# Two transformer blocks on one core: conditioning vectors made by VectorE row sums in place of small matmuls, with one more buffer per weight ring and new pool starts

## The chip, the cores and the metric

The kernel runs on one core of a Trainium2 chip. The metric is device time in microseconds (us), from the first to the last instruction of the core with what lies around it. All arithmetic is float32; TensorE takes its operands as pairs of rounded floats (fp32r).

## The reference, cut to what matters

Two blocks follow each other on 512 tokens of width 1024. The first has two layers; each norm in it is scaled, shifted and gated by six vectors that a matrix product makes from one conditioning row (`c` for the tokens, `c_ctx` for 256 context tokens):

```
sc  = silu(c);  scc = silu(c_ctx)
for l in range(2):
    shift1, scale1, gate1, shift2, scale2, gate2 = split(sc @ w_mod[l] + b_mod[l], 6)    # w_mod[l] is 1024 x 6144
    ...                                       the same six from scc for the context
    xn = rms_norm(x, g_norm1[l]) * (1 + scale1) + shift1
    mix = concat(attention, fourier, conv, pool)(xn @ w_in[l]) @ w_out[l]
    x = x + gate1 * mix
    xn = rms_norm(x, g_norm2[l]) * (1 + scale2) + shift2
    x = x + gate2 * ((silu(xn @ w_a) * (xn @ w_g)) @ w_ffn_out)       # inner width 2816
```

The second block has a retention and convolution layer and a latent attention layer, without conditioning.

## The kernel before, in words

Activations lie transposed: 128 features by up to 512 tokens. Every weight tile is loaded as `raw` (SyncE issues all loads), split into a rounded part `wh` (ScalarE or VectorE) and a rest `wl` (VectorE), and each product is three matmuls (`mm3`): wh with xh, wh with xl, wl with xh. `raw` has a ring of 4 buffers, `wh` and `wl` of 3 each.

The order of all instructions is not written out. The program is recorded as operations with a due time, and a planner (`Rec.order`) lays them out with its own cost figures, due times (`SHIFTS`, `MOD0`, `LATE` and others in `CFG`), penalties for moving an elementwise operation to another engine (`PEN_...`), and the order of the output columns of each projection (`STEPS`). What it lays out is fixed: each engine runs its list in order, and SyncE issues its loads in order.

Conditioning ("modulation") is made in 12 blocks of 512 columns per layer, `mod_block(l, b)`: eight 128x512 pieces of `w_mod` come in (tiles `mraw` or `raw`), and eight matmuls `md<-mraw,scp` with the silu'd conditioning (`scp`, 32 columns, of which two carry data) as the stationary operand write four 32-row strips of one PSUM bank, in two groups of four matmuls each; the profile counts each of these plain fp32 matmuls twice, so a group shows as x8. ScalarE copies the bank (`mrow`), four transposes `md<-cst,mrow` turn it, a VectorE reduce writes `modT`, two more small operations add the bias and make the scale `sclT`. Blocks 0 to 3 of layer 0 come first of all, blocks 4 to 11 of layer 0 during its mixers (`NMOD`), and the 12 of layer 1 during the feed-forward of layer 0 (`ffn`), one after every second inner tile. Block 10 and 11 of a layer are the gate of its feed-forward; the first `fo` result that is added to `x` needs block 10.

The feed-forward makes inner tiles by pairs: `fa` and `fg` products (512 token columns and 256 context columns in layer 0), silu on ScalarE (`ft`), product and split (`hh`, `hl`, `hid`), then the product `fo` for each group of 5 to 8 inner tiles. Names of tiles: `yxh`, `yxl`, `yc` are the normed inputs, `xt` and `ct` the residual streams.

Pools are stacked from the two ends of the on-chip memory: constants, `spt` (365 columns of small parameters), the weight rings and the rings `a` and `b` on one side; `pp` (attention) and then `pa2` (feed-forward) on the other. The starts of the rings follow from the sizes ahead of them: by the built program every tile of the rings `raw`, `wh`, `wl`, `a` and `b` starts 32 bytes past a multiple of 128, those of `pp` and `pa2` 96 bytes past one.

Of the kernel before, what the change touches and what calls it, by code (L numbers as in the profile page):

```python
# [8 lines left out]
F32 = mybir.dt.float32  # L9
# [7 lines left out]
P = 128  # L17
D = 1024
# [32 lines left out]
def win_cols():  # L51
    out = {}
    ar = np.arange
    for c in range(2):
# [17 lines left out]
     'LATEM': 26000.0,  # L72
# [8 lines left out]
     'PEN_PE': (0, 150, None),  # L81
# [10 lines left out]
     'WOE': 3,  # L92
     'WOK': (3, 0, 2, 7, 5, 4, 6, 1),
     'WOS': 7,
# [8 lines left out]
     'PEN_CP': (0, 0, None),  # L103
     'PEN_CZ': (0, 0, None),
     'PEN_PE': (0, 0, None),
# [18 lines left out]
     'PEN_RND': (0, None, None),  # L124
     'PEN_SQ': (None, 0, None),
# [8 lines left out]
     'backlog': 0,  # L134
     'table_slack': 504.2099999999999,
     'urgent': 11068.417919999998},
 3: {'PEN_ADD': (0, None),
     'PEN_AFF': (0, 0, None),
     'PEN_CP': (0, 0, None),
# [15 lines left out]
     'backlog': 0,  # L155
# [2120 lines left out]
```

## Time and profile before

| | |
|---|---|
| median of 3 runs | 2245.21 us (2242.07 to 2246.84) |
| the profiled execution | 2242.23 us, span 2240.2 us |
| TensorE | busy 2134.7 us of the span, 12922 matmul records, mean granted clock 0.98 |
| VectorE, ScalarE | busy 1418.0 and 866.7 us |
| DMA | 258.4 MB, 115 GB/s over the span |

An engine's busy time counts each instruction from its start to its end; matmuls overlap each other, so for TensorE the step from one start to the next says more than the length of one. By stages, all times from the start of the span: the first 56 us load and norm; layer 0's mixers run to about 280, its output projection to about 360, its feed-forward to about 956; layer 1's mixers to about 1120, projection and feed-forward to about 1536; the second block takes the rest.

### The profile page before, as it was taken

The page shows a single profiled execution, that of the slowest core. Times are in us where ns is not written, and L with a number is a line of the kernel's source. Part 1 is how long each engine was busy: PE and PEld are TensorE (multiplying, and loading weights), DVE is VectorE, ACT ScalarE, POOL GpSimd, SP SyncE. Part 2 cuts the span into 40 slices and gives each one's busy share as a digit, 9 for nine tenths or more (in the row PEclk, how much of TensorE's full clock was granted, in tenths as well). Part 3 has the DMA queues.
Part 4 walks back from the last instruction along what each step waited for, and adds up shares of the span by engine and source line. Part 5 has one row for each costly group of instructions (what it writes and reads, how often), then busy time and mean ns, then how long its engine had stood idle before and what let it go on. Part 6 is the DMA issues. An engine that isn't in the chain of part 4 may idle for free.

```text
span 2240.2 us, 32559 instructions
## 1 busy us (share of the span) xinstructions
PE 2134.7 (95%) x12922; PEld 1845.7 (82%) x12922; DVE 1418.0 (63%) x2671; ACT 866.7 (39%) x1646; POOL 22.2 (1%) x35
## 2 busy tenths in 40 slices
PE   7799999999999999888899999999999999999997
PEld 3477799888888888777798888888888888989887
DVE  6998886332232232899984333459775685787996
ACT  6457754111212111664852212215341341435662
POOL 0001000000000000000100000000000000000000
PEclk9799999999999999998999999999999999999998
DMA  8225464222331423422043232335323224543223
GB/s 306 98 98 181 161 217 137 76 98 67 125 101 60 148 78 120 145 89 90 20 142 95 96 110 94 113 117 162 104 85 99 90 89 121 166 139 113 66 77 123
DMA packets 87176, 258.44 MB, mean 115 GB/s; under 512 B 10480, under 2 KB 18160, under 8 KB 87024
## 3 DMA queue, kind: packets, MB, share of 16 engines
q1 hardware_dynamic: 87024, 256.36, 35.7%
q8 instruction: 101, 1.65, 0.3%
q14 instruction: 51, 0.42, 0.1%
HBM read 249.24 MB, written 2.10 MB: 112 GB/s over the span
## 4 chain that ended last, share of the span: by engine, by line
PE 77%; DVE 14%; ACT 4%; DMA 2%; issue 2%; SPq 1%; DVEq 0%; ACTq 0%
PE fa L1001 14%; PE fg L1001 14%; PE fo L1001 13%; PE y L1001 5%; PE wi L1001 5%; PE wo L1001 4%; PE gt L1001 2%; PE egc L1001 2%; PE md L1001 2%; DVE wl L1001 2%; PE ecb L1001 2%; PE ecx L1001 2%; PE ecc L1001 2%; PE egr L1001 2%; DVE cy L1001 1%
## 5 line engine op out<-in xcount | busy, mean ns | idle before, releaser
L1001 DVE TENSOR_TENSOR wl<-raw,wh 128x1024 fp32r<-128x1024 f32 (+5 forms) x387 | 434.6, 1125 | 41.4 <-ACT wh L1001 28.9
L1001 ACT CAST wh<-raw 128x1024 fp32r<-128x1024 f32 (+4 forms) x224 | 216.7, 970 | 417.4 <-PE fo L1001 197.4
L1001 DVE CAST wh<-raw 128x1024 fp32r<-128x1024 f32 (+4 forms) x163 | 105.3, 646 | 211.8 <-PE fa L1001 73.7
L1001 DVE TENSOR_TENSOR ft<-ft,fg 128x256 f32<-128x256 f32 (+1 forms) x66 | 39.4, 598 | 270.7 <-PE fg L1001 270.7
L1001 PE MATMUL fo<-hh,wl 128*128 128x512 f32 (+1 forms) x448 | 156.5, 349 | 6.7 <-DVE wl L1001 6.7
L1001 PE MATMUL fo<-hh,wh 128*128 128x512 f32 (+1 forms) x448 | 157.8, 352 | 0.0
L1001 PE MATMUL fo<-hl,wh 128*128 128x512 f32 (+1 forms) x448 | 157.2, 351 | 0.0
L1001 PE MATMUL fa<-yxh,wh 128*128 128x512 f32 (+1 forms) x384 | 144.9, 377 | 0.0
L1001 PE MATMUL fg<-yxh,wh 128*128 128x512 f32 (+1 forms) x384 | 144.4, 376 | 0.0
L1001 PE MATMUL fa<-yxl,wh 128*128 128x512 f32 (+1 forms) x384 | 143.9, 375 | 0.2 <-DVE yxl L1001 0.2
L1001 PE MATMUL fg<-yxl,wh 128*128 128x512 f32 (+1 forms) x384 | 143.9, 375 | 0.0
L1001 PE MATMUL fa<-yxh,wl 128*128 128x512 f32 (+1 forms) x384 | 142.8, 372 | 0.0
L1001 PE MATMUL fg<-yxh,wl 128*128 128x512 f32 (+1 forms) x384 | 142.7, 372 | 0.0
L1001 PE MATMUL y<-mxh,wl 128*128 128x256 f32 x384 | 110.9, 289 | 6.1 <-DVE wl L1001 6.1
L1001 PE MATMUL y<-mxh,wh 128*128 128x256 f32 x384 | 111.8, 291 | 4.7 <-DVE wh L1001 3.3
L1001 PE MATMUL y<-mxl,wh 128*128 128x256 f32 x384 | 110.1, 287 | 0.3 <-DVE mxl L1001 0.3
L1001 ACT ACTIVATE ft<-fa 128x256 f32<-128x256 f32 (+1 forms) x66 | 34.2, 526 | 178.1 <-PE fa L1001 178.1
L1001 PEld LDWEIGHTS fo<-hh,wl 128*128 128x128 f32 x448 | 85.9, 192 | 18.6 <-DVE wl L1001 7.1
L1001 PEld LDWEIGHTS fo<-hh,wh 128*128 128x128 f32 x448 | 85.4, 191 | 8.4 <-issue 1.7
L1001 PE MATMUL wi<-xxh,wh 128*128 128x512 f32 (+1 forms) x240 | 90.5, 377 | 1.6 <-DVE c L1001 0.7
L1001 PE MATMUL wi<-xxh,wl 128*128 128x512 f32 (+1 forms) x240 | 86.5, 360 | 5.3 <-DVE wl L1001 5.3
L1001 PEld LDWEIGHTS fo<-hl,wh 128*128 128x128 f32 x448 | 86.3, 193 | 5.6
(457 smaller groups left out, 5910.5 us busy)
## 6 DMA issues: line engine op xcount, KB each, us to landing
raw<-in_w SPq DMA_DIRECT2D x291, 512.0 KB, 3.6
mraw<-in_wm SPq DMA_DIRECT2D x48, 512.0 KB, 4.8
raw<-in_wm SPq DMA_DIRECT2D x32, 512.0 KB, 4.8
raw<-in_w SPq DMA_DIRECT2D x24, 448.0 KB, 3.4
raw<-in_w SPq DMA_DIRECT2D x32, 320.0 KB, 3.1
mraw<-in_wm SPq DMA_DIRECT2D x32, 256.0 KB, 5.9
raw<-in_w SPq DMA_DIRECT2D x16, 384.0 KB, 3.1
rw<-rt SPq DMA_DIRECT2D x76, 64.0 KB, 2.0
```

The costliest lines, as they stand in the source:

```text
L1001: getattr(engs[o.eng], method)(*[real(a) for a in args], **{k: real(v) for k, v in kw.items()})
```

## The change

- `mod_rows` replaces `mod_block` for the 12 blocks of layer 1 and for blocks 10 and 11 of layer 0 (`MODV`), which move from the mixers into the feed-forward. The weights of these blocks are stored transposed (`wt`): four tiles of 128 outputs by 1024 inputs for a block. For each, VectorE multiplies the tile by the conditioning row, which lies on all 128 partitions (`crow`, 2 x 1024), and sums along the row: three instructions with a summed output, two of 512 columns for `c` (into `mj`, thrown away) and one of 1024 for `c_ctx`. `crow` is loaded by a broadcast and silu'd by ScalarE when the feed-forward's pool opens. The ring `mraw` of these tiles has one buffer (`NMR`) of 512 KB, where it had two.
- The rings `raw`, `wh` and `wl` have one buffer more (5, 4, 4). The scratch for DMAs issued by GpSimd shrinks to 1 KB per partition; GpSimd issues none.
- Three pads (`spt` 40 columns longer, a 24-column tile on the right side, 544 columns for the wide tiles of `pp`) move the starts: by the built program the rings `raw`, `wh`, `wl`, `a` and `b` now start at multiples of 256 bytes, those of `pp` and `pa2` at odd multiples of 128.
- New settings: due times, penalties, the order in `STEPS` of both layers of the second block, where two projections (`q0`, `t7`) are no longer made in two halves with a load and split of their own each; several others (`k1`, `g5`, `g7`) are made in one piece of 512 columns in place of two of 256.

```diff
 CFG (cut: some twenty values, among them)
-     'LATEM': 26000.0,
+     'LATEM': 25000.0,
-     'WOE': 3,
+     'WOE': 1,
-     'WOS': 7,
+     'WOS': 6,
-     'STEPS': [('q0', '0'), ('g1', '0'), ('k0', '0'), ('g6', 'x'), ('k0', '1'), ('q0', '1'), ('g0', 'x'),
+     'STEPS': [('q0', '01'), ('g1', '0'), ('k0', '0'), ('g6', 'x'), ('g0', 'x'), ('k1', 'x'), ('k0', '1'),
...
+MODP = 10
+MODV = [(0, b) for b in range(MODP, 12)] + [(1, b) for b in range(12)]
...
-    wm = np.stack([inp["w_mod"][l].reshape(2, 4, P, 6144)[..., b].transpose(0, 2, 1, 3)
-                   for l in range(2) for b in MODB])
+    wm = np.stack([inp["w_mod"][0].reshape(2, 4, P, 6144)[..., b].transpose(0, 2, 1, 3) for b in MODB[:MODP]])
+    wt = np.stack([inp["w_mod"][l][:, MODB[b]].T.reshape(4, P, D) for l, b in MODV])
...
-        return self.A(nm=nm) if n <= 512 else self.pp.tile([P, n], F32, tag="w", bufs=4, name=self.name(nm))
+        return self.A(nm=nm) if n <= 512 else self.pp.tile([P, 544], F32, tag="w", bufs=4, name=self.name(nm))[:, :n]
...
-        h = self.pw.tile([P, 1024], F32R, tag="wh", bufs=3, name=self.name("wh"))
-        lo = self.pw.tile([P, 1024], F32R, tag="wl", bufs=3, name=self.name("wl"))
+        h = self.pw.tile([P, 1024], F32R, tag="wh", bufs=4, name=self.name("wh"))
+        lo = self.pw.tile([P, 1024], F32R, tag="wl", bufs=4, name=self.name("wl"))
...
+    def mod_rows(self, l, b):
+        nc = self.nc
+        m4 = self.modT[l][:, b]
+        e = self.col(4)
+        def dot(o, t, c, v, at):
+            nc.vector.scalar_tensor_tensor(o, t[:, c], 1.0, self.crow[:, v, c], op0=ALU.mult, op1=ALU.mult, accum_out=at)
+        for i in range(4):
+            t = self.pa2.tile([P, D], F32, tag="mraw", bufs=self.NMR, name=self.name("mraw"))
+            nc.sync.dma_start(out=t, in_=self.aps["wt"][MODV.index((l, b)), i])
+            o = self.A(nm="mj")
+            dot(o, t, slice(0, 512), 0, m4[:, i, 0:1])
+            dot(o, t, slice(512, D), 0, e[:, i:i + 1])
+            dot(t, t, slice(0, D), 1, m4[:, i, 1:2])
+        nc.vector.tensor_tensor(m4[:, :, 0:1], m4[:, :, 0:1], e.rearrange("p (a o) -> p a o", o=1), op=ALU.add)
+        self.mod_end(l, b)
...
                 if l == 0 and j % 2 == 0 and j < 24:
-                    self.mod_block(1, j // 2)
-                if l == 0 and j % 2 == 1 and self.NMOD + j // 2 < 8:
-                    self.mod_block(0, 4 + self.NMOD + j // 2)
+                    self.mod_rows(1, j // 2)
+                if l == 0 and j % 2 == 1 and MODP + j // 2 < 12:
+                    self.mod_rows(0, MODP + j // 2)
...
+            if self.nph == 2:
+                self.crow = self.pa2.tile([P, 2, D], F32, tag="crow", bufs=1, name="crow")
+                self.nc.sync.dma_start(out=self.crow, in_=self.aps["cr"].rearrange("o (v k) -> o v k", v=2).to_broadcast([P, 2, D]))
+                self.nc.scalar.activation(self.crow, self.crow, AF.Silu)
...
-    NA, NB, NRAW = 53, 11, 4
+    NA, NB, NRAW = 53, 11, 5
+    NA2, NMR = 14, 1
...
-        t = self.psm.tile([P, 8, 2], F32, tag="sc", bufs=1, name="sc")
+        t = self.ptop.tile([P, 24], F32, name="sc")[:, :16].rearrange("p (k v) -> p k v", v=2)
...
-            self.spt = pc.tile([P, nsp], F32, name="spt")
+            self.spt = pc.tile([P, nsp + 40], F32, name="spt")[:, :nsp]
...
-    nc = _bacc.Bacc("TRN2", target_bir_lowering=False, num_devices=1)
+    nc = _bacc.Bacc("TRN2", target_bir_lowering=False, num_devices=1, dynamic_dma_scratch_size=1024)
```

What the planner makes of it shows in three places. On TensorE, in the feed-forward of layer 0, the kernel before puts half a modulation block and its transposes between products of an inner tile (`fa`, `yxh` and `yc` as above):

```order
L1001 MATMUL fa_6117<-yxl_3951,wh_5978 128x512
L1001 MATMUL fa_6117<-yxh_3941,wl_5996 128x512
L1001 MATMUL md_6096<-mraw_6113,scp 32x512 x2
L1001 MATMUL md_6096<-mraw_6129,scp 32x512 x2
L1001 MATMUL fa_6107<-yc_3620,wh_5978 128x256 x2
L1001 MATMUL fa_6107<-yc_3620,wl_5996 128x256
L1001 MATMUL fa_6117<-yxh_3946,wh_5978 128x512
L1001 MATMUL fa_6117<-yxl_3958,wh_5978 128x512
L1001 MATMUL fa_6117<-yxh_3946,wl_5996 128x512
L1001 MATMUL md_1154_6165<-cst,mrow_6160 128x128 x4
L1001 MATMUL fa_6117<-yxh_3964,wh_5978 128x512
```

In the changed program such a stretch holds products alone; no `md` row is left on TensorE after the mixers of layer 0. On VectorE, at the start of that feed-forward, the list before (here the first inner tile) has splits of weights, products and splits of hidden tiles:

```order
L1001 TENSOR_TENSOR ft_4207<-ft_4207,fg_4209 128x256
L1001 TENSOR_TENSOR hid_4360<-ft_4207,hid_4360 128x256
L1001 CAST wh_4378<-raw_4121 128x1024
L1001 TENSOR_TENSOR ft_4334<-ft_4334,fg_4225 128x512
L1001 TENSOR_TENSOR wl_4391<-raw_4121,wh_4378 128x1024
L1001 TENSOR_TENSOR hl_4404<-ft_4334,hh_4396 128x512
```

The changed list has row sums among them, here two tiles of block 11 of layer 0:

```order
L1004 SCALAR_TENSOR_TENSOR mj_4784,modT_306<-mraw_4759,crow 128x512
L1004 TENSOR_TENSOR ft_4719<-ft_4719,fg_4715 128x512
L1004 SCALAR_TENSOR_TENSOR mj_4784,c_4796<-mraw_4759,crow 128x512
L1004 TENSOR_TENSOR wl_4803<-raw_4399,wh_4786 128x1024
L1004 TENSOR_TENSOR hl_4813<-ft_4719,hh_4801 128x512
L1004 SCALAR_TENSOR_TENSOR mraw_4759,modT_306<-mraw_4759,crow 128x1024
L1004 SCALAR_TENSOR_TENSOR mj_4854,modT_306<-mraw_4831,crow 128x512
L1004 SCALAR_TENSOR_TENSOR mj_4854,c_4796<-mraw_4831,crow 128x512
L1004 TENSOR_TENSOR wl_4871<-raw_4466,wh_4856 128x1024
L1004 SCALAR_TENSOR_TENSOR mraw_4831,modT_306<-mraw_4831,crow 128x1024
```

The sums stand wherever the planner found VectorE free by its own figures: the first 4 tiles during the output projection, 16 more ahead of the first `ct<-fo`, the other 36 over the rest of the feed-forward. On SyncE the loads of that stretch alternate:

```order
L1004 DMA mraw_4633<-in_wt 128x1024
L1004 DMA raw_4669<-in_w 128x768
L1004 DMA mraw_4696<-in_wt 128x1024
L1004 DMA raw_4731<-in_w 128x768
L1004 DMA mraw_4759<-in_wt 128x1024
```

Each `mraw` load waits for the last sum of the tile before it, and the weight load that follows stands behind it. In the program before, two `mraw` loads stand together and then three or four weight loads.

## Rows read from the trace of the kernel before

**Rows 1.** Busy time by stage: PE, PEld, DVE, ACT, POOL busy (instructions), clock, DMA.
```profile
56.00:280.00 224.00, 199.75 (x1179) 156.03 (x1178) 200.96 (x454) 140.05 (x275) 13.32 (x14) 0.92 0.40 134
280.00:392.00 112.00, 110.25 (x894) 103.62 (x894) 82.87 (x166) 55.59 (x113) 0.00 (x0) 1.00 0.54 177
392.00:896.00 504.00, 504.00 (x2909) 424.75 (x2909) 149.11 (x228) 90.92 (x144) 0.00 (x0) 1.00 0.29 97
1512.00:2240.00 728.00, 696.37 (x4428) 630.17 (x4426) 549.81 (x1048) 292.33 (x594) 0.00 (x0) 0.98 0.36 110
```
**Rows 2.** PE in time, half a block: start us, us, engine, line, operation, tiles, count.
```profile
451.02 0.39 PE L1001 MATMUL fa<-yxh,wl 128*128 128x512 f32 x1
451.34 1.07 PE L1001 MATMUL md<-mraw,scp 128*32 128x512 f32 x8
452.34 0.50 PE L1001 MATMUL fa<-yxh,wh 128*128 128x512 f32 x1
452.68 0.39 PE L1001 MATMUL fa<-yxl,wh 128*128 128x512 f32 x1
452.91 0.40 PE L1001 MATMUL fa<-yxh,wl 128*128 128x512 f32 x1
```
**Rows 3.** PE in time, the four transposes of a block.
```profile
442.53 0.39 PE L1001 MATMUL fg<-yxh,wl 128*128 128x512 f32 x1
442.76 0.60 PE L1001 MATMUL md<-cst,mrow 128*128 128x128 f32 x4
443.12 0.48 PE L1001 MATMUL fg<-yxh,wh 128*128 128x512 f32 x1
443.43 0.39 PE L1001 MATMUL fg<-yxl,wh 128*128 128x512 f32 x1
```
**Rows 4.** Tile md from 290 to 910 us: count, duration ns min/median/max, first and last start.
```profile
L1001 PE MATMUL md<-mraw,scp x192: 592/605/617, 297.4 to 905.0; 128*32 128x512 f32 x192
L1001 PE MATMUL md<-cst,mrow x48: 270/272/275, 335.1 to 907.0; 128*128 128x128 f32 x48
```
**Rows 5.** DVE by line and form: count, busy us, mean ns of one, idle before.
```profile
L1001 DVE TENSOR_TENSOR wl<-raw,wh 128x1024 fp32r<-128x1024 f32 x291 | 354.7, 1221 | 17.0 <-ACT wh L1001 5.6 <-DVE wh L1001 0.5
L1001 DVE TENSOR_TENSOR hl<-ft,hh 128x512 fp32r<-128x512 f32 x44 | 30.1, 684 | 0.0
L1001 DVE RECIPROCAL c<-c 128x1 f32<-128x1 f32 x72 | 11.0, 154 | 2.8 <-ACT pe L1001 2.6
```
**Rows 6.** ACT, tile c: how ScalarE writes a summed output.
```profile
L1001 ACT ACTIVATION_READ_ACCUMULATOR pe<-sc,c,rq x40: 186/192/233, 166.2 to 1121.9; 128x1 f32 x40
```
**Rows 7.** DMA issues: count, KB each, median us from issue to landing.
```profile
raw<-in_w SPq DMA_DIRECT2D x291, 512.0 KB, 3.6
mraw<-in_wm SPq DMA_DIRECT2D x48, 512.0 KB, 4.8
```
**Rows 8.** What PE waited for: us in total, times, longest.
```profile
PE fo L1001 <- DVE wl L1001: 11.1, 3, 4.3
PE y L1001 <- DVE wl L1001: 6.1, 4, 2.2
PE wi L1001 <- DVE wl L1001: 5.3, 2, 4.1
PE y L1001 <- DVE wh L1001: 3.3, 2, 1.6
PE lat L1001 <- DVE wl L1001: 2.7, 1, 2.7
```
**Rows 9.** PE in time, feed-forward of layer 1: steps of 512-column products from two rings.
```profile
1239.64 0.39 PE L1001 MATMUL fg<-yxh,wh 128*128 128x512 f32 x1
...
1241.91 0.39 PE L1001 MATMUL fa<-yxl,wh 128*128 128x512 f32 x1
...
1299.87 0.40 PE L1001 MATMUL fo<-hh,wh 128*128 128x512 f32 x1
...
1301.50 0.40 PE L1001 MATMUL fo<-hl,wh 128*128 128x512 f32 x1
```

More of the change, by code (lines that the diff above doesn't have):

```diff
@@ L80 @@
      'PEN_CZ': (0, 0, None),
-     'PEN_PE': (0, 150, None),
+     'PEN_PE': (0, 0, None),
      'PEN_RND': (0, None, None),
@@ L102 @@
      'PEN_CA': (0, None),
-     'PEN_CP': (0, 0, None),
+     'PEN_CP': (300, 0, None),
      'PEN_CZ': (0, 0, None),
-     'PEN_PE': (0, 0, None),
+     'PEN_PE': (0, 300, None),
      'PEN_RND': (0, 1000, None),
@@ L123 @@
      'PEN_PE': (0, 0, None),
-     'PEN_RND': (0, None, None),
-     'PEN_SQ': (None, 0, None),
+     'PEN_RND': (0, 150, None),
+     'PEN_SQ': (300, 0, None),
      'PEN_SUB': (0, None),
@@ L128 @@
      'PEN_WL': (0, None),
[5 rows of a table removed]
-     'backlog': 0,
-     'table_slack': 504.2099999999999,
-     'urgent': 11068.417919999998},
[5 rows of a table added]
+     'backlog': 1.5,
+     'table_slack': 2722.7339999999995,
+     'urgent': 29884.72838399999},
  3: {'PEN_ADD': (0, None),
-     'PEN_AFF': (0, 0, None),
-     'PEN_CP': (0, 0, None),
+     'PEN_AFF': (0, 300, None),
+     'PEN_CP': (0, 300, None),
      'PEN_PE': (0, 0, None),
@@ L145 @@
      'PEN_WL': (0, None),
[7 rows of a table removed]
[6 rows of a table added]
      'YE': 1,
      'YS': 4,
-     'backlog': 0,
+     'backlog': 0.25,
      'table_slack': 338.9702987999999,
@@ L158 @@
 SHIFTS = {'mla': 10000.0,
- 'ret': 12000.0,
+ 'ret': -8000.0,
  (0, 'c', 'attn'): 7000.0,
- (0, 'c', 'conv'): 39000.0,
- (0, 'c', 'four'): 16000.0,
+ (0, 'c', 'conv'): 42000.0,
+ (0, 'c', 'four'): 11000.0,
  (0, 'c', 'pool'): 43000.0,
- (0, 'c', 'taps'): -92000.0,
+ (0, 'c', 'taps'): -115000.0,
  (0, 'x', 'attn'): -3000.0,
- (0, 'x', 'conv'): 48000.0,
+ (0, 'x', 'conv'): 56000.0,
  (0, 'x', 'four'): 19000.0,
@@ L171 @@
  (1, 'x', 'conv'): 63000.0,
- (1, 'x', 'four'): -6000.0,
- (1, 'x', 'pool'): 84000.0,
+ (1, 'x', 'four'): -3000.0,
+ (1, 'x', 'pool'): 83000.0,
  (1, 'x', 'taps'): 25000.0}
@@ L387, in pack @@
     arrays = {
-        "w": np.concatenate(w.parts), "wm": np.ascontiguousarray(wm),
+        "w": np.concatenate(w.parts), "wm": np.ascontiguousarray(wm), "wt": np.ascontiguousarray(wt),
+        "cr": np.ascontiguousarray(np.concatenate([inp["c"].reshape(1, D), inp["c_ctx"].reshape(1, D)], axis=1)),
         "sp": np.ascontiguousarray(np.concatenate(parts, axis=1)),
@@ L1040 @@
     FOC = None
-    NMOD = 8
     def __init__(self, rec, aps, w_at, sp_at):
@@ L1261, in mod_block @@
                     t = self.A(nm="mraw")
-                elif self.pm2 is None:
+                else:
                     t = self.raw()
-                else:
-                    t = self.pa2.tile([P, 1024], F32, tag="mraw", bufs=2, name=self.name("mraw"))
                 t = t.rearrange("p (a c) -> p a c", a=w)
                 at = q * w
-                nc.sync.dma_start(out=t, in_=self.aps["wm"][l * 12 + b, half, :, at:at + w])
+                nc.sync.dma_start(out=t, in_=self.aps["wm"][b, half, :, at:at + w])
                 got += [(at + i, t[:, i]) for i in range(w)]
@@ L1280, in mod_block, with mod_end @@
         nc.vector.tensor_reduce(m4, p2.rearrange("p (a j q) -> p a q j", a=4, j=4)[:, :, 0:2, :], axis=AX.X, op=ALU.add)
+        self.mod_end(l, b)
[13 more added lines that the diff above has]
+        nc.vector.tensor_tensor(m4[:, :, 0:1], m4[:, :, 0:1], e.rearrange("p (a o) -> p a o", o=1), op=ALU.add)
+        self.mod_end(l, b)
+    def mod_end(self, l, b):
+        nc = self.nc
+        m4 = self.modT[l][:, b]
         bm = self.S(("bmod", l))[:, 4 * b:4 * b + 4]
@@ L1785, in ffn @@
         if l == 0:
-            self.mod_block(1, 11)
+            self.mod_rows(1, 11)
             self.pm2 = None
@@ L1809, in phase @@
             self.pm2 = pool("pm2", bufs=4, space=PSUM)
-            self.pa2 = pool("pa2", bufs=19 if self.nph > 2 else 14, side="right")
+            self.pa2 = pool("pa2", bufs=19 if self.nph > 2 else self.NA2, side="right")
+            if self.nph == 2:
+                self.crow = self.pa2.tile([P, 2, D], F32, tag="crow", bufs=1, name="crow")
+                self.nc.sync.dma_start(out=self.crow, in_=self.aps["cr"].rearrange("o (v k) -> o v k", v=2).to_broadcast([P, 2, D]))
+                self.nc.scalar.activation(self.crow, self.crow, AF.Silu)
     def close_phase(self):
@@ L1845, in first_layer @@
                     px(c)
-            for i in range(self.NMOD):
+            for i in range(MODP - 4):
                 with nc.shift(self.MOD0 + self.MODD * i):
@@ L2239, in run @@
             self.nph = 0
+            self.ptop = pool("top", bufs=1, side="right")
             self.pm = pool("pm", bufs=4, space=PSUM, reuse_waits="tile")
```

21 rows, old and new, of the table CFG are left out of this document.

## The prediction

> **What bounds the kernel now.** I read the busy times by stage first. In the 504 us from 392 to 896, the feed-forward of layer 0, TensorE is busy without a gap, while VectorE works 149.1 us and ScalarE 90.9 us [rows 1]. In the output projection (280 to 392) TensorE has 110.3 of 112 us. In the first mixers (56 to 280) TensorE and VectorE share the bound, 199.8 and 201.0 of 224 us. The second block from 1512 on is at 696.4 of 728 us on TensorE. So whatever leaves TensorE in the feed-forward shortens the kernel one for one, and VectorE has 355 us of room there. The second view is TensorE's own order in time: what a modulation block really takes there is the step to the next product, not the length of its records [rows 2, 3]. The third are TensorE's waits: five groups on VectorE's splits make 28.5 us in the whole program [rows 8].
>
> The profiled execution took 2242.23 us; the median is 2245.21, 3.0 more. The sum goes from the execution, and the 3.0 are added at the end. A measurement here can tell a change from none at about 0.2%, 4.5 us.
>
> **The change part by part.**
>
> 1. *The 12 blocks of layer 1 leave TensorE.* Half a block stands between the product at 451.02 and the one at 452.68: 1.66 us, of which two ordinary steps of 0.23 belong to the products (452.68 to 452.91 is one), so 1.20 us [rows 2]. The transposes stand between 442.53 and 443.43: 0.90 less 0.46 is 0.44 us [rows 3]. A block is 2 x 1.20 + 0.44 = 2.84 us. The 192 records of `mraw` matmuls (16 a block) and 48 transposes (4 a block) are just 12 blocks [rows 4], lying between 297 and 907 us where TensorE is full: 12 x 2.84 = **-34.1 us**.
>
> 2. *Blocks 10 and 11 of layer 0 leave the mixers.* 2 x 2.84 = 5.7 us of TensorE, which idles 24 of 224 us there [rows 1]; VectorE and ScalarE lose a `modT` reduce and a copy each, well under a microsecond a block. Between 0 and -5.7 I take the middle, **-3**.
>
> 3. *The row sums on VectorE.* 14 blocks of 4 tiles, each two sums of 512 columns and one of 1024. No row of before has such an instruction. The nearest two-input ones take 684 ns for 128x512 and 1221 for 128x1024 [rows 5]: 2 x 0.684 + 1.221 = 2.59 us a tile if writing out the sum is free. ScalarE writes a summed output with a further instruction of 192 ns [rows 6], and a 128x1 operation of VectorE takes 154 ns; at 0.19 for each of three a tile is 3.16 us. I take 3.16: 56 x 3.16 = 177 us, some 145 without the reads. The Trainium skill ("VectorE: DVE Perf Modes", section "Two Vector instructions with no wait between them") says that an operation that also writes out its accumulator is two instructions; by that the upper value holds, and no run so far shows it for VectorE. 52 of the tiles lie in the feed-forward: 164 us more, 149 + 164 = 313 of the 470 us that remain after part 1. VectorE does not become full, so this costs nothing **by its amount**.
>
>  What can cost is the order. The ring of these tiles has one buffer, so each load waits for the last sum on the tile before, the weight load behind it on SyncE waits too, and the next sum, at its fixed place in VectorE's list, stands until the load has landed. A load lands in 3.6 us (`raw`) to 4.8 us (`mraw`, in two pieces a row) [rows 7]; the new tiles are whole rows like `raw`, so I take 3.6. Other VectorE work, 149/52 = 2.9 us a tile, lies under the landing. A tile then cycles in 3.6 + 3.16 = 6.8 us (8.0 at 4.8), 52 of them in 352 us (414), under 470. The first 16 are packed ahead of the first `fo` additions. They need 16 x 6.8 = 108 us; TensorE reaches that point after some six inner tiles, each 48 products of 512 columns at 0.227 [rows 9] and 48 of half that, 16.4 us, so 98 us. The shortage is 10 us (29 at 4.8), partly covered by weights already split: **+4**, bounds 0 and +29.
>
> 4. *The first 4 tiles and `crow` in the output projection.* VectorE has 82.9 of 112 us there and gets 4 x 3.16 = 12.6 [rows 1]; it still fits, but TensorE has 2 us of slack and the 1 MB broadcast and its Silu (two or more times a 512 KB load) stand on SyncE and ScalarE. Bounds 0 and +12.6; **+3**.
>
> 5. *Deeper rings.* One more tile of each of `raw`, `wh`, `wl` lets SyncE and VectorE run one weight (24 products, some 5 us) further ahead. The five waits on splits are 11.1 + 6.1 + 5.3 + 3.3 + 2.7 = 28.5 us, the longest 4.3 [rows 8]. Each is shorter than 5 us, so all could go; but a ring helps only where VectorE had time earlier, and these stand at the joints of stages, where the split's own input order decides. Bounds 0 and -28.5; nearer to a quarter, **-8**.
>
> 6. *Halves merged in `STEPS`.* Two splits and two loads fewer, and pairs of 256-column products made into one of 512: **-1**. The other settings (due times, penalties) only shift operations among engines; none shows a size, bounds -10 to +10, **0**.
>
> 7. *Starts of the rings.* Work is the same. Rows show that TensorE's step for 512 columns is 0.227 us when operands are in ring `a` (1239.64 to 1241.91, ten steps) and 0.233 when they are in `pa2` (1299.87 to 1301.50, seven steps) [rows 9]; these rings differ in their start (32 and 96 bytes past a multiple of 128), and also in what is multiplied. So a start may matter by 6 ns. VectorE shows nothing of it: its times go by columns alone [rows 5]. I take **0**; bounds are 6 ns on the 4,608 products of 512 columns of the changed program, +28 and -28. By the Trainium skill ("SBUF — State Buffer", section "Specifications (TRN2)") on-chip memory works in 16-byte lines; both old and new starts are multiples of 16, so by that rule the pads would change nothing at all and the term is 0. The two steps here lie in rings that are both multiples of 16 and differ, so the trace doesn't settle it.
>
> Sum: -34.1 - 3 + 4 + 3 - 8 - 1 + 0 = **-39**: 2242.2 - 39.1 = 2203.1 on the execution's scale, **2206 us** on that of the median.
>
> **The rivals.**
>
> *R1, the one-buffer ring makes VectorE the bound: slower.* If the planner's list leaves little between the last sum of a tile and the first of the next, VectorE stands through each landing and its other work comes on top: 52 x (4.8 + 3.16) + 149 = 563 us for the feed-forward, where TensorE had 504. That is +59 in place of -34 and of the +4; with -9 from parts 2, 4, 5 and 6 it is +50: **2295 us**. It decides from a landing at which 52 x (L + 3.16) + 149 passes 504 + 9: L = 3.8 us, between the two rows. For it: the list shows some tiles back to back with only one split between, and SyncE's weight loads queue behind. Against: most of the 36 later tiles have other work between. 0.11.
>
> *R2, given back.* The same with landings of 3.6: 52 x 6.76 + 149 = 501, as long as before; only the -9 stays: **2236 us**. 0.12.
>
> *R3, the starts speed TensorE up.* If every 512-column step falls by the 6 ns that separate the two rings now, 4,608 x 6 ns = 28 us: 2206 - 28 = **2178**; with as much again from the rest (7,106 products of 256 columns at half, 21 us, and -8 from settings) about 2150. For it: the two steps differ at clock 1.00 with TensorE full. Against: different operands; VectorE is indifferent. 0.17.
>
> *R4, nothing comes of it*: the gain of part 1 is eaten by the terms with a plus at their upper bounds, +29 and +12.6 against -34.1 and the -12 of parts 2, 5 and 6: about -4, **2241**. 0.04.
>
> **How the numbers follow.** The forecast has 0.56, R3 0.17, R2 0.12, R1 0.11, R4 0.04. The forecast's own range is 2190 to 2225, from half the deeper-ring bound on one side and the order's on the other. The range to hold the time 8 in 10 goes from R3's far end, 2150, to just beyond R2, 2238; R1, R4 and the lowest part of R3 are left out. Faster by over 0.2% (below 2240.7): forecast, R3 and R2, 0.85. Within: R4, 0.04. Slower: R1, 0.11.
>
> **What would show it.** Part 1: no `md` row on TensorE after 290 us and a feed-forward of layer 0 about 34 us shorter. Part 3: VectorE busy some 300 us in that feed-forward; a sum pair of 0.68 and 1.22 us with reads of 0 to 0.19; TensorE's waits on VectorE's `hh`, `wl` or `ct` there of a few us. R1 and R2: VectorE idle before `mj` released by the DMA of `mraw`, over 150 us, and TensorE waiting behind `wl` for tens of us. Part 5: the groups of [rows 8] down by about 8 us. R3: the two steps of [rows 9] below 0.227 and 0.233, and stages without any modulation, the second block above all, shorter. The prediction is wrong if the second block changes by more than 15 us, since I give it only the rings' few us, or if a row sum is over 0.2 us longer than a product of its size.

## The result, and the profile after

The changed kernel takes 2160.41 us (2159.80 to 2162.77) against 2244.47 (2242.07 to 2246.84): a ratio of 0.9627, 95% interval 0.9611 to 0.9644, 84 us faster. The forecast was 2206, 39 us faster: the direction was right and the time lies in the range given, but the gain is more than twice the one forecast.

Where it came from is read best from the lengths of stages. A stage ends here with a product on TensorE: **A** ends with the first `fa` product of the feed-forward of layer 0 (load, mixers and output projection lie in it), **B** with the last `fo` of layer 0, **C** with the last `wo` of layer 1, **D** with the last `fo` of layer 1, **E** with the last `ecx` (first layer of the second block), **F** with the last instruction. In us, from the start times in the two traces:

| | A | B | C | D | E | F | span |
|---|---|---|---|---|---|---|---|
| before | 356.5 | 599.3 | 210.6 | 370.0 | 339.5 | 364.4 | 2240.2 |
| after | 334.6 | 567.4 | 203.3 | 363.7 | 339.4 | 348.3 | 2156.6 |
| difference | -21.9 | -31.9 | -7.3 | -6.3 | 0.0 | -16.1 | -83.6 |

B is the feed-forward that the modulation left, and its 31.9 us are close to the 30.1 of the prediction's parts 1 and 3. That is partly luck: in the kernel before, TensorE makes only some 10 of the 12 blocks in stage B, and the first ones in the output projection, stage A (from 356.4 to 956 us; count, duration, first and last start):

```profile
L1001 PE MATMUL md<-mraw,scp x152: 592/605/617, 439.9 to 905.0; 128*32 128x512 f32 x152
L1001 PE MATMUL md<-cst,mrow x40: 270/272/275, 442.8 to 907.0; 128*128 128x128 f32 x40
```

The other 51.7 us lie in stages for which the prediction's parts have 9, or 16 with the blocks put where they were.

Busy time in stage B of the changed kernel (PE, PEld, DVE, ACT, POOL busy, instructions in brackets, clock, DMA share, GB/s):

```profile
334.60:902.00 567.40, 562.41 (x3404) 501.75 (x3403) 344.87 (x700) 154.76 (x260) 0.21 (x4) 0.99 0.39 123
```

TensorE is still all but full, VectorE has gone to 344.9 us. Before, in the same stage from 356.5 to 955.8, TensorE had 590.8 of 599.3 us and VectorE 220.9.

The row sums, by line and form on VectorE (count, busy us, mean ns of one, idle before):

```profile
L1004 DVE SCALAR_TENSOR_TENSOR mj<-mraw,crow 128x512 f32<-128x512 f32 x112 | 77.2, 690 | 85.9 <-DMA mraw<-in_wt 84.3
L1004 DVE SCALAR_TENSOR_TENSOR mraw<-mraw,crow 128x1024 f32<-128x1024 f32 x56 | 68.4, 1221 | 1.1
L1004 DVE DVE_READ_ACCUMULATOR mj<-mraw,crow 128x1 f32 x112 | 9.2, 82 | 0.0
L1004 DVE DVE_READ_ACCUMULATOR mraw<-mraw,crow 128x1 f32 x56 | 4.6, 81 | 0.0
```

A tile's records make 2 x (0.690 + 0.082) + 1.221 + 0.081 = 2.85 us of VectorE, between the 2.59 and 3.16 of the prediction. Writing out the sum is a second instruction. The Trainium skill has it so too ("VectorE: DVE Perf Modes", section "Two Vector instructions with no wait between them"), and the trace agrees, with 168 such reads. But a read takes 82 ns where ScalarE's takes 192 [rows 6], and in order of time (start us, us; idle time before) most of it is hidden:

```profile
386.15 0.69 DVE L1004 SCALAR_TENSOR_TENSOR mj<-mraw,crow 128x512 f32<-128x512 f32 x1 [1.44 <-DMA mraw<-in_wt]
386.77 0.08 DVE L1004 DVE_READ_ACCUMULATOR mj<-mraw,crow 128x1 f32 x1
386.77 1.22 DVE L1004 TENSOR_TENSOR wl<-raw,wh 128x1024 fp32r<-128x1024 f32 x1
...
393.63 0.69 DVE L1004 SCALAR_TENSOR_TENSOR mj<-mraw,crow 128x512 f32<-128x512 f32 x1 [0.74 <-DMA mraw<-in_wt]
394.25 0.08 DVE L1004 DVE_READ_ACCUMULATOR mj<-mraw,crow 128x1 f32 x1
394.37 0.69 DVE L1004 SCALAR_TENSOR_TENSOR mj<-mraw,crow 128x512 f32<-128x512 f32 x1
```

A split starts together with the read; only a further sum stands 0.12 us behind it. The 84.3 us in the list are VectorE standing for the load of the one-buffer ring, 41 times.

What TensorE waited for (us, times, longest), the rows of after that answer to [rows 8] and the two largest:

```profile
PE cm L1004 <- DVE cy L1004: 21.5, 2, 21.1
PE ss L1004 <- DVE sq L1004: 15.1, 2, 9.8
...
PE fo L1004 <- DVE wl L1004: 5.1, 3, 2.5
...
PE y L1004 <- DVE wl L1004: 1.7, 2, 1.1
```

The five groups of [rows 8] fell from 28.5 us to 5.1 + 1.7 = 6.8; `y` on `wh`, `wi` on `wl` and `lat` on `wl` are gone. But `cm` on `cy` grew to 21.5 us from this:

```profile
PE cm L1001 <- DVE cy L1001: 4.8, 2, 3.9
```

All of TensorE's waits together fell only from 94.9 to 79.6 us, so most of the 84 us are not waits that went. No wait on a row sum is among them.

The loads (KB each, median us from issue to landing):

```profile
raw<-in_w SPq DMA_DIRECT2D x289, 512.0 KB, 3.6
mraw<-in_wt SPq DMA_DIRECT2D x56, 512.0 KB, 3.4
```

Whole rows land like `raw`, as assumed, not like the `mraw` of [rows 7].

TensorE's steps, in the feed-forward of layer 1, the stretches that answer to [rows 9]:

```profile
1176.41 0.39 PE L1004 MATMUL fg<-yxh,wh 128*128 128x512 f32 x1
...
1178.68 0.39 PE L1004 MATMUL fa<-yxl,wh 128*128 128x512 f32 x1
...
1207.08 0.40 PE L1004 MATMUL fo<-hh,wh 128*128 128x512 f32 x1
...
1208.46 0.39 PE L1004 MATMUL fo<-hh,wh 128*128 128x512 f32 x1
```

The `fa` and `fg` products step by 2.27/10 = 0.227 us, exactly as before. The `fo` products step by 1.38/6 = 0.230, where they had 0.233. Over all such products of layer 1 the means are 0.227 before and after for `fa` and `fg` (some 320 steps each), and 0.2335 and 0.2289 for `fo` (339 and 338).

### The profile page after: what moved, and what is told of

It is laid out like the page before. It is cut to its first block, busy times and chain, and to the rows that moved or that the text cites. A ratio compares the mean times of both kernels' runs of the same rounds, so it can differ in the third digit from the quotient of the medians.

```text
span 2156.6 us, 32192 instructions
## 1 busy us (share of the span) xinstructions
PE 2065.9 (96%) x12570; PEld 1814.0 (84%) x12570; DVE 1508.8 (70%) x2943; ACT 910.6 (42%) x1697; POOL 20.6 (1%) x35
## 4 chain that ended last, share of the span: by engine, by line
PE 77%; DVE 14%; ACT 4%; DMA 2%; issue 2%; SPq 1%; DVEq 0%; ACTq 0%
PE fa L1004 14%; PE fg L1004 14%; PE fo L1004 13%; PE y L1004 6%; PE wi L1004 3%; PE wo L1004 3%; DVE cy L1004 2%; PE gt L1004 2%; DVE wl L1004 2%; PE egc L1004 2%; PE ecb L1004 2%; PE ecc L1004 2%; PE egr L1004 2%; PE ecx L1004 2%; PE sc L1004 2%
## 5 line engine op out<-in xcount | busy, mean ns | idle before, releaser
L1004 ACT CAST wh<-raw 128x1024 fp32r<-128x1024 f32 (+5 forms) x270 | 260.9, 973 | 418.8 <-PE fo L1004 177.7
L1004 DVE CAST wh<-raw 128x1024 fp32r<-128x1024 f32 (+5 forms) x115 | 73.9, 644 | 141.4 <-PE ecx L1004 18.3
L1004 DVE SCALAR_TENSOR_TENSOR mj<-mraw,crow 128x512 f32<-128x512 f32 x112 | 77.2, 690 | 85.9 <-DMA mraw<-in_wt 84.3
L1004 DVE SCALAR_TENSOR_TENSOR xt<-fo,modT,xt 128x512 f32<-128x512 f32 (+1 forms) x72 | 44.9, 628 | 61.8 <-PE fo L1004 61.6
```

Source lines behind the costliest of these rows:

```text
L1004: getattr(engs[o.eng], method)(*[real(a) for a in args], **{k: real(v) for k, v in kw.items()})
```

## Experiments

Two questions: which part of the change gave the 52 us outside stage B, and whether the parts that came out near the forecast did so for the reason given. First each part alone on the kernel before, then each part taken out of the changed kernel. Stage lengths of the first eight runs stand in one table behind them. Each run was timed beside the kernel before, which took 2240.8 to 2244.5 us from one session to the next, and the ratios below are to that. A difference to the changed kernel's 2160.41 us, which belongs to the first session, is therefore good to 3 or 4 us.

**1. The rings alone, on the kernel before.**

```diff
-    NA, NB, NRAW = 53, 11, 4
+    NA, NB, NRAW = 53, 11, 5
-        ... tag="wh", bufs=3     ... tag="wl", bufs=3
+        ... tag="wh", bufs=4     ... tag="wl", bufs=4
-    nc = _bacc.Bacc("TRN2", ...)
+    nc = _bacc.Bacc("TRN2", ..., dynamic_dma_scratch_size=1024)
```

> The kernel before with the rings raw, wh and wl one buffer deeper (and the smaller GpSimd scratch that pays for them), nothing else changed. The change gained 84 us, of which 32 lie in the feed-forward of layer 0, where the modulation left TensorE; 52 us lie elsewhere (22 before that feed-forward, 7 in layer 1's mixers, 6 in its feed-forward, 16 in the last stage). T1 (deeper rings gave the 52): about 2195 us, 45 to 55 faster, with TensorE's waits on wl and wh nearly gone. T2 (the new settings gave them): 2237, the 8 us of the prediction. T3 (the new starts gave them): 2237 as well.

Measured: 2226.72 us against 2242.65, ratio 0.9919 (0.9900 to 0.9938). 16 us: neither T1's 45 to 55 nor the prediction's 8.

**2. The new settings alone, on the kernel before** (all of `CFG` and `SHIFTS`, with `STEPS`).

> The kernel before with the new values in CFG and SHIFTS and the new order of STEPS alone. T1 (rings): 2244, within 5 us of before. T2 (settings): 2195 to 2210, most of it before the feed-forward of layer 0 and in the last stage. T3 (starts): 2244.

Measured: 2257.16, ratio 1.0059 (1.0038 to 1.0079). The settings alone make the kernel *slower* by 14.5 us. T2 falls in this form, and so does the "within 5 us" of the other two.

**3. The row sums alone** (`mod_rows` for the 14 blocks, rings, settings and starts as before).

> The kernel before with the row sums alone: 14 blocks by mod_rows, one mraw buffer, rings, settings and starts as before. The prediction's parts 1 to 4 give -34.1 - 3 + 4 + 3 = -30: 2214 us. Under T1, T2 and T3 alike 2205 to 2216. If the row sums themselves also relieve the mixers and the last stage (T4, a gain of the moved blocks that was mis-sized), 2195 or less.

Measured: 2222.61, ratio 0.9900 (0.9880 to 0.9920), 20 us, 7 us beyond the range that three theories shared, and T4 falls. Stage B is 27.6 us shorter, but the output projection within A is 7 us longer and stage C 9.7.

**4. The starts alone** (the three pads).

```diff
-            self.spt = pc.tile([P, nsp], F32, name="spt")
+            self.spt = pc.tile([P, nsp + 40], F32, name="spt")[:, :nsp]
...
```

> The kernel before with the three pads alone (and the smaller scratch), so that the rings raw, wh, wl, a and b start at the changed kernel's multiples. T1 and T2: 2244, within 4 us, with TensorE's steps of 512 columns at 0.227 to 0.233 us. T3 (starts): 20 us or more faster, with shorter steps in every stage.

Measured: 2237.40, ratio 0.9973 (0.9960 to 0.9986), 5 us. T3 falls as the source of the 52 us. The smaller scratch, which runs 1 and 3 have too, was not tried alone; run 7 keeps it. The trace shows where some of the 5 us can be: of the products looked at (`fa`, `fg`, `fo`, `ecx`) only `fo` changed its step. Here they are, in order of time, the stretch that answers to the second half of [rows 9]:

```profile
1294.70 0.39 PE L1001 MATMUL fo<-hh,wl 128*128 128x512 f32 x1
...
1296.30 0.39 PE L1001 MATMUL fo<-hh,wh 128*128 128x512 f32 x1
```

1.60/7 = 0.229 us, where the same products took 0.233 before; over the 768 `fo` products of 512 columns that is 3 us. The pads alone do it: the mean of layer 1's `fo` steps is 0.2335 before and 0.2289 here, and without the pads (run 7) it is 0.2334 again.

Alone the four parts add to -16 + 14.5 - 20 - 5 = -27 us, and together they give -84. So 57 us were an interaction, and the next four runs take one part each *out* of the changed kernel.

**5. The changed kernel with the old settings.**

> The changed kernel with the old values in CFG, SHIFTS and STEPS. Alone, rings gave -16, rows -20, starts -5 and settings +14.5; these add to -27, the change gave -84, so 57 us are an interaction. T5 (the new settings pay only in the program they stand in, where rings or rows are there): with the old ones it falls to the sum of the other three, 2195 to 2205. T6 (rings and rows together are worth more than apart, the settings are a matter of a few us): 2150 to 2175.

Measured: 2238.99, ratio to before 0.9984 (0.9971 to 0.9998). Nearly the whole gain is gone, and the time is 34 us beyond T5's range. Three quarters of the loss are in one place: stage C has 261.7 us instead of 203.3. Another 13 are in stage A.

**6. The changed kernel with rings of 4, 3 and 3.**

> The changed kernel with rings of 4, 3 and 3. T5, if the settings rest on the deeper rings: 2210 to 2240 (rows and starts, and the settings' loss); if they rest on the rows: 2175 to 2185. T6: 2190 to 2215, since both sides of the pair are needed.

Measured: 2220.21, 0.9899 (0.9883 to 0.9915), 60 us slower than the changed kernel, spread over all stages but B (+1). That is within T5's range for settings that rest on the rings, and 5 us beyond T6's.

**7. The changed kernel without the pads.**

> The changed kernel without the three pads. From the pads alone (5 us): 2165 in all theories. If the starts carry a part of the interaction, 2175 or more.

Measured: 2163.83, 0.9652 (0.9634 to 0.9669), 3.4 us, about what the starts gave alone. They take no part in the interaction.

**8. Everything but the row sums** (rings, settings and pads on the kernel before).

> The kernel before with rings, settings and starts, all modulation on TensorE as before. T5, if the settings rest on the rings: 2185 to 2195 (the change less the 20 to 32 us of the rows); if on the rows: 2225 to 2235. T6: 2220 to 2235.

Measured: 2199.89, 0.9811 (0.9796 to 0.9826). Rings, settings and starts give 43.0 us, and the row sums added to them another 39.5 (to 2160.41). The time is 5 us above T5's range for settings that rest on the rings, and far from the other two. The settings lose 14.5 us on the old rings and gain some 22 on the new ones without any row sums (43.0 less the 16 of run 1 and the 5 of run 4). But with the row sums there too, taking the settings out costs 79 us (run 5): 58 of them are a stage C that neither the rings (207.1) nor the rows (220.3) bring about by themselves. So what the settings are worth rests on the rings, and the larger part of it on rings and rows together.

| run | A | B | C | D | E | F |
|---|---|---|---|---|---|---|
| before | 356.5 | 599.3 | 210.6 | 370.0 | 339.5 | 364.4 |
| 1 rings | 348.7 | 600.3 | 207.1 | 368.5 | 346.4 | 355.0 |
| 2 settings | 354.1 | 599.2 | 218.6 | 370.4 | 347.8 | 363.7 |
| 3 rows | 355.3 | 571.7 | 220.3 | 370.0 | 339.4 | 364.1 |
| 5 after, old settings | 347.5 | 565.5 | 261.7 | 366.9 | 344.9 | 353.4 |
| 6 after, old rings | 356.5 | 568.7 | 211.1 | 370.3 | 346.1 | 365.6 |
| 8 after, no rows | 339.2 | 599.0 | 205.9 | 363.7 | 340.6 | 348.7 |
| after | 334.6 | 567.4 | 203.3 | 363.7 | 339.4 | 348.3 |

Runs 4 and 7 are left out: they differ by at most 1.4 us in any stage from the kernel before and the changed one. Column B answers to the row sums above all (599 to 600, or 566 to 572). Column F answers to the rings first (364 or 353 to 355) and then to the settings (another 5 to 6). Stage E is the one in which rings or settings without the other do harm (345 to 348), and both together none or next to none.

**9. The changed kernel with the old settings of layer 1's mixers alone**, to find the 58 us of run 5.

```diff
  CFG[1]
-     'PEN_CP': (300, 0, None), 'PEN_PE': (0, 300, None)
+     'PEN_CP': (0, 0, None),   'PEN_PE': (0, 0, None)
  SHIFTS
-  (1, 'x', 'four'): -3000.0, (1, 'x', 'pool'): 83000.0
+  (1, 'x', 'four'): -6000.0, (1, 'x', 'pool'): 84000.0
```

> The changed kernel with the old values of layer 1's own settings alone (two penalties and five due times of its mixers). With all settings old, layer 1's mixers took 262 us where the change has 203, and TensorE did the attention heads there one after the other with little between them. T7 (a planner's accident of layer 1's own settings with the deeper rings and the row sums): 2215 to 2222, all of the loss between the last fo of layer 0 and the last wo of layer 1. T8 (it comes from the settings of other stages): 2160 to 2165.

Measured: 2216.43, 0.9884 (0.9870 to 0.9899), and stage C is 260.0 us, the others within 1.4 us of the changed kernel. (The expectation speaks of five due times; two of them differ.) T7 stands in place and size: two penalties and two due times are worth 56 us in this program. Why the planner lays out the chain so with the old ones was not traced. TensorE in order of time in this run, in the middle of stage C (start us, us; in brackets the idle time before and what ended it):

```profile
1077.12 1.12 PE L1004 MATMUL pt<-cst,pe 128*128 128x128 f32 x4 [0.91 <-DVE ao L1004]
1079.69 0.69 PE L1004 MATMUL pt<-cst,pe 128*128 128x128 f32 x2 [1.46 <-DVE ptl L1004]
1081.55 0.80 PE L1004 MATMUL sc<-kh,qs 128*128 128x512 f32 x1 [1.17 <-ACT pe L1004]
1082.14 0.63 PE L1004 MATMUL sc<-kl,qs 128*128 128x512 f32 x1
1082.57 0.41 PE L1004 MATMUL sc<-kh,qs 128*128 128x256 f32 x1
1082.78 0.41 PE L1004 MATMUL sc<-kl,qs 128*128 128x256 f32 x1
1083.00 1.05 PE L1004 MATMUL pt<-cst,pe 128*128 128x128 f32 x4
1085.45 0.69 PE L1004 MATMUL pt<-cst,pe 128*128 128x128 f32 x2 [1.40 <-DVE ptl L1004]
```

An attention head is a chain: scores `sc`, softmax, transposes `pt`, split `ptl`, values `pv`. Here nothing stands between its links and TensorE idles 0.9 to 1.5 us at each. In the changed kernel products of the output projection do:

```profile
1040.33 0.60 PE L1004 MATMUL pt<-cst,pe 128*128 128x128 f32 x4
1040.68 0.36 PE L1004 MATMUL wo<-mxh,wh 128*128 128x256 f32 x1
1040.88 0.28 PE L1004 MATMUL wo<-mxl,wh 128*128 128x256 f32 x1
1041.00 0.28 PE L1004 MATMUL wo<-mxh,wl 128*128 128x256 f32 x1
1041.12 0.40 PE L1004 MATMUL sc<-kh,qs 128*128 128x512 f32 x1
1041.35 0.40 PE L1004 MATMUL sc<-kl,qs 128*128 128x512 f32 x1
```

What does run is slower there, too. By windows of 60 us, first run 9 from 1082, then the changed kernel from 1022:

```profile
1082.00:1142.00 60.00, 40.69 (x232) 35.05 (x232) 29.82 (x54) 17.83 (x36) 0.00 (x0) 0.70 0.18 59
```

```profile
1022.00:1082.00 60.00, 57.18 (x441) 53.72 (x440) 57.35 (x125) 50.13 (x94) 0.00 (x0) 1.00 0.22 71
```

The granted clock is 0.70 against 1.00, so of its two levels (1.2 and 2.4 GHz) TensorE is at the lower one for some 60% of the stretch. It was 1.00 from 1060 to 1070 us, where TensorE was busy 7.2 of 10 us, 0.52 in the next 10 and 0.50 in those after, and 1.00 again from 1130 on, where TensorE is busy without a gap. At the lower level the step from 1082.14 to 1082.57, a `sc` of 512 columns, takes 0.43 us; in the changed kernel (1041.12 to 1041.35) it takes 0.23.

**10. The changed kernel with the second block's old settings.**

> The changed kernel with the old settings of the second block (both layers' STEPS, penalties and due times). From the stage lengths of the run with all settings old (5 us in its first layer, 5 in its second): 2170, with the first layer 345 and the second 341 us long. If the second block's settings are worth what they were on the kernel before (a loss of 7): 2153.

Measured: 2172.30, 0.9687 (0.9672 to 0.9701), stages E 344.6 and F 352.3: 5 and 4 us, as expected, and another 3 in D. (The 341 us of the expectation do not run to the end of stage F.)

**11. The changed kernel with a `raw` ring of 4, and 12. with `wh` and `wl` rings of 3.**

> The changed kernel with a raw ring of 4 (wh and wl stay at 4). Without all three extra buffers it took 2220, 60 us more. T9 (the load's lead is what counts): 2200 to 2220. T10 (the splits' lead counts, raw is free soon after its split): 2160 to 2170. T11 (a chain of three rings is as deep as its shallowest): 2200 or more here and in the next run.

> The changed kernel with wh and wl rings of 3 (raw stays at 5). T9: 2160 to 2175. T10: 2200 to 2220. T11: 2200 to 2220 as well.

Measured: 2189.87 (0.9764, 0.9745 to 0.9782) and 2213.24 (0.9872, 0.9856 to 0.9887): 29 and 53 us more than the changed kernel. No theory stands as written: T9 misses both runs, T10 and T11 the first one. The splits' lead is worth the most, but `raw` is not free of cost either. Where they lose differs: run 11 in A (347.9) and C (222.0) and almost nowhere else (F 350.4), run 12 in all (348.8, 570.3, 213.4, 371.5, 344.0, 362.1). Run 12's waits of TensorE:

```profile
PE wi L1004 <- DVE wl L1004: 22.9, 2, 17.3
...
PE fo L1004 <- DVE wl L1004: 12.6, 4, 4.3
PE wo L1004 <- DVE wl L1004: 9.6, 3, 3.6
...
PE y L1004 <- DVE wl L1004: 7.3, 5, 3.4
...
PE lat L1004 <- DVE wl L1004: 2.2, 1, 2.2
```

These are 54.6 us of waits on `wl`; the changed kernel has 7.9 (the 6.8 above and 1.1 for `wo`). Not all of the 47 us between are the fourth buffer's. The longest, 17.3 us, ends at 111 us, where the changed kernel waits 21.1 us for `cy`: VectorE is all but full there in both (27.8 and 29.0 of the 29 us from 80 to 109), and only the tile that TensorE waits for differs. Without it, waits on `wl` grew by 29 us, in `fo`, `wo`, `y` and the first `wi`. All waits of TensorE together grew from 79.6 to 113.1, 33.5 of the 53 us.

**13. Blocks 10 and 11 of layer 0 back on TensorE.**

```diff
-MODP = 10
+MODP = 12
```

> The changed kernel with blocks 10 and 11 of layer 0 made on TensorE in the mixers, as before; layer 1's blocks stay with VectorE. If their TensorE time is all (2 x 2.84 us), the first mixers take 243 to 246 us and the kernel 2163 to 2166; if they cost what adding the row sums gave there, 247.6 and 2168; if the order around them did it, within 2 us of 2160.

Measured: 2163.85, 0.9645 (0.9631 to 0.9660), 3.4 us slower, within the first range. Stage A is 337.2 in place of 334.6. The first mixers (up to the first `wo`) missed it: they take 249.1 us where the changed kernel has 239.5, and the output projection takes 88.2 in place of 95.1, so 7 us of work changed its place between the two. A worth of 3 us, as the prediction has it, fits; it is no more than the sessions differ.

**14. The changed kernel with layer 0's old settings.**

> The changed kernel with layer 0's own old settings. The run with all settings old had 245 us in the first mixers and 102 in the output projection, where the change has 240 and 95: 2172 if these are layer 0's own. If they come from the settings of other stages: 2160.

Measured: 2171.38, 0.9675 (0.9660 to 0.9689): 11 us, with stage A at 346.9, as expected.

**15. The context convolution of layer 0 later.** In the changed kernel the largest wait of TensorE, 21.1 us, is on `cy` in the first mixers.

```diff
- (0, 'c', 'conv'): 42000.0,
+ (0, 'c', 'conv'): 65000.0,
```

> The changed kernel with the context convolution's due time 23000 later, so that its product on TensorE (cm) stands behind most of the input projection instead of ahead of it. If the 21 us wait on it is on the path, TensorE has input products to do meanwhile and the first mixers get 10 to 20 us shorter: 2140 to 2150. If VectorE is the bound of that stretch (it is busy all of it), the wait turns up behind other products and the time stays within 5 us of 2160.

Measured: 2172.37, 0.9677 (0.9661 to 0.9693): 12 us slower, a miss of both sides. The wait fell to 9.2 us, but stage A grew from 334.6 to 351.9. VectorE's part of the reasoning stands: from 80 to 120 us it is busy without a gap in both kernels, and TensorE has 15.0 us of the 40 before the edit and 20.9 behind it.

```profile
80.00:120.00 40.00, 15.05 (x77) 9.31 (x76) 40.00 (x81) 11.88 (x22) 0.00 (x0) 0.66 0.33 108
```

```profile
80.00:120.00 40.00, 20.93 (x84) 10.71 (x83) 40.00 (x82) 13.14 (x23) 0.00 (x0) 0.66 0.46 150
```

The 6 us that TensorE does earlier are lost later on: 8 of 40 us are idle from 160 to 200, where the changed kernel has one. Making the wait shorter was no gain here, but since the edit moved much else, the run doesn't show that it couldn't be one. Why the later order is 17 us worse in stage A was not followed up.

**16 and 17. The sums made two and three times**, to see how near the slower rival was.

```diff
             dot(o, t, slice(0, 512), 0, m4[:, i, 0:1])
             dot(o, t, slice(512, D), 0, e[:, i:i + 1])
+            dot(o, t, slice(0, 512), 0, m4[:, i, 0:1])
+            dot(o, t, slice(512, D), 0, e[:, i:i + 1])
             dot(t, t, slice(0, D), 1, m4[:, i, 1:2])
```

> The changed kernel with the two 512-column sums of each tile made twice: 1.55 us more on VectorE a tile (4.4 in place of 2.85), 81 us in the feed-forward of layer 0, where it was busy 345 of 567 us. If room on VectorE is what counts (its work is then 426 of 567, and a tile's cycle 3.4 + 4.4 = 7.8 us, 52 of them 406): within 8 us of 2160. If the ring binds as the rival had it, with nothing of the other work under the loads: 52 x 7.8 + 165 = 571, a few us more than now, 2165 to 2175; the first part, 16 tiles packed ahead of the first additions, would show it first.

> The same sums made three times: 3.1 us more a tile (5.95), 161 us in the feed-forward: VectorE's work is 506 of 567 us, a tile's cycle 9.35 us, 52 of them 486. If room counts: 2165 to 2180. If the ring binds with nothing under the loads: 52 x 9.35 + 165 = 651, 84 us more: 2235 to 2245.

Measured: 2160.48 (0.9628, 0.9612 to 0.9644) and 2207.13 (0.9835, 0.9816 to 0.9855). Making them twice adds 78 us to VectorE's busy time in stage B and costs nothing; three times adds 144 us and costs 47, of which 31 in stage B and 16 in C. Stage B by windows, twice and then three times:

```profile
336.10:901.90 565.80, 560.69 (x3404) 500.23 (x3403) 422.54 (x931) 149.10 (x256) 0.21 (x4) 1.00 0.37 123
```

```profile
337.50:936.30 598.80, 567.96 (x3407) 505.28 (x3406) 489.30 (x1148) 153.47 (x260) 0.21 (x4) 0.97 0.36 118
```

TensorE's wait of the tripled run that appears in that stage:

```profile
PE fo L1004 <- DVE wl L1004: 28.2, 8, 14.1
```

VectorE at 423 of 566 us delays nothing; at 489 it splits weights too late for `fo`. The truth for three lies between the two expectations: part of the other work does lie under the loads.

## Why the prediction was right and wrong

**Part 1 and the amount of part 3: right; the order of part 3: not seen.** No `md` product is on TensorE after 235 us (the mixers of layer 0). At the prediction's prices the 152 matmuls and 40 transposes that stood in stage B make 9.5 x 2.40 + 10 x 0.44 = 27.2 us, and the row sums alone took 27.6 off it (run 3). In run 8 more of them stand there, from 339.2 to 938.3 us:

```profile
L1000 PE MATMUL md<-mraw,scp x176: 592/605/617, 388.8 to 889.9; 128*32 128x512 f32 x176
L1000 PE MATMUL md<-cst,mrow x48: 270/272/273, 355.5 to 891.9; 128*128 128x128 f32 x48
```

These are 31.7 us, and from run 8 to the changed kernel, which differ in the row sums alone, B went from 599.0 to 567.4, -31.6. So the price of a block holds in both pairs, and nothing is left for the +4 of the order. The prediction had placed all 12 blocks in the feed-forward; 6.9 of its 34.1 us lay in the output projection, and rings, settings and starts took some 4.7 us off stage B. That -30.1 is near -31.9 is these errors cancelling.

VectorE got busier by 345 - 221 = 124 us, where 52 x 3.16 = 164 were counted. The records of the sums make 153.0 us there, but records of neighbours overlap, and of rounding `wh` VectorE keeps 4.3 of 15.1 us (ScalarE has 15 more). That the ring of one buffer holds VectorE up was right too (84 us of standing), and that TensorE hardly feels it. Runs 16 and 17 place the bound: it decides somewhere between a tile of 4.4 and one of 5.95 us of VectorE, so R1 and R2 had no place at 2.85 us with a landing of 3.4. The prediction's point for R1, a landing of 3.8, left out that other work fills the landing, as its own "against" said.

**Part 2: not contradicted.** -3 forecast, 3.4 by run 13, which is no more than the sessions differ.

**Part 4: within its bounds, and what it costs rests on the order around it.** +3 forecast. With the rows alone (run 3) 12.6 us of modulation left stage A (the 6.9 above and two blocks of 2.84), but it became only 1.2 us shorter: 11.4 went back, and the output projection grew from 101 to 109 us. With rings and new settings (run 8 to the changed kernel) 2.8 + 5.7 us left, and it became 4.6 shorter: 3.9 went back, some of it idle time that part 2 had allowed for.

**Parts 5 and 6: the step that failed.** Rings and settings had -8, -1 and 0, each priced by itself and added. Together, without the pads, they gave 43.0 - 3.4 = 39.6 us, 31 more than forecast. That is most of the 45 us by which the forecast was short; the rest are the row sums in the finished program (39.5 in place of 30) and the starts (3.4 in place of 0). Three things were wrong.

First, the rings. Alone they gave 16 us, twice the 8 (run 1), and "nearer to a quarter" of the 28.5 us of [rows 8] is not how. TensorE's waits in run 1:

```profile
PE wi L1001 <- DVE wl L1001: 14.7, 2, 13.3
PE fo L1001 <- DVE wl L1001: 7.5, 3, 2.8
...
PE y L1001 <- DVE wl L1001: 3.5, 4, 1.0
```

In stage F the waits of `y` and `lat` went from 12.1 to 3.8 us, most of the 9.4 that F lost. There the reason given, that VectorE had no time earlier at the joints of stages, does not hold: its work in F is the same within 1% (288.5 and 286.2 us). But `wi` went up from 5.3 to 14.7, so the five groups together only fell to 26.0. Its long wait ends at 109 us, behind a stretch in which VectorE is busy all of the time (29.0 of the 29 us from 80 to 109), and the changed kernel waits 21.1 us for `cy` at the same place. So the fall of the five groups from 28.5 to 6.8 us is partly a wait that goes by another name.

Second, the settings were priced at 0 within +/-10 since "none shows a size". A setting has no duration of its own, but it sets which work lies between the links of a chain: with the old values for layer 1's mixers the changed kernel loses 56 us, with those of layer 0 another 11, with those of the second block 12.

Third, the parts were added. The settings lose 14.5 us on the old rings and gain some 22 on the new ones: the planner finds another order whenever a ring changes, and they keep the gain of the rings from being lost to a bad one. No row of before could give that size.

What the 39.6 us are made of is shown in part only. In F of the changed kernel TensorE's idle time fell from 26.9 to 15.1 us, its busy time by 4.3, while the granted clock rose from 0.97 to 0.99. In A, the largest, TensorE's idle time did not fall at all (42.6 to 48.6 us): its busy time fell by 27.9 us, of which 12.6 are modulation. What shortened the other 15 was not followed up.

**Part 7 and R3: inside its bounds, for one group of products only.** Starts are worth 3.4 to 5 us. In layer 1 `fa` and `fg`, whose moving operand is in ring `a`, did not change (0.227); `fo` went from 0.233 to 0.229. The prediction read the two steps as those of two rings, which they are not quite: `hh` lies in `pa2`, but `hl` of layer 1 in ring `a` by the kernel. And in layer 0 `fa` and `fg`, from ring `a` as well, step by some 0.234 with and without the pads, so the start of a ring is not all that sets a step. The rule of the Trainium skill that was weighed there ("SBUF — State Buffer", section "Specifications (TRN2)", lines of 16 bytes) would have given no change at all; the measurement speaks against it as the whole story, since both starts are multiples of 16. R3's 28 us are refuted: most of the products kept their step.

**The last sign given**, that the prediction is wrong if the second block changes by more than 15 us, was met: E and F together lost 16.1 us, from the rings (F 364.4 to 355.0, run 1) and the settings that go with them (F 348.7 in run 8, which has no row sums).

## What to carry to other kernels

For a deeper ring, ask at each wait on its tiles whether the producer has time *before* it: where it has (`y` and `lat` here), the wait can go; where it is busy without a gap, the wait stays, if under the name of another tile. The list of waits by tile alone does not tell these apart, and here it bounded the gain neither way. Where a planner lays out the order, an edit of a buffer or a due time changes the whole program, so its parts can't be added: test the set together, compare stage lengths, and look for chains that lost their filler. Before going after a large wait in the list, look whether the engine waited for is itself full there: in run 15 it was, and moving the work gained nothing.

## What the runs showed of the hardware

VectorE's read of an accumulated sum has a record of 82 ns, less than half of ScalarE's 192, and a sum of 512 columns 690 ns, what a plain product of two inputs takes (684). From start to start a sum with its read takes 0.62 us before an instruction of another kind (median of 39), where a plain product of 512 columns takes 0.60, and 0.74 us before another sum (393.63 to 394.37): so the read costs almost nothing unless sums follow each other.

With pads that moved the rings `raw`, `wh`, `wl`, `a` and `b` from 32 bytes past a multiple of 128 to multiples of 256, and `pa2` from 96 bytes past one to odd multiples of 128, TensorE's step for the `fo` products of 512 columns in layer 1 fell from 0.233 to 0.229 us (runs 4 and 7), and the 0.227 of `fa` and `fg` did not change. Which of the moves does it, and what in the address, was not tried.
